# A fused hybrid block: work in front of the scan moves from GpSimd to VectorE, cross-attention queries come first, and two transposes wait longer

## The chip, the cores and the metric

The kernel runs as one launch on one core of a Trainium2 chip. The metric is the device time of that launch in microseconds. Three runs of the kernel before took 1974.82 to 1976.23 us, with a median of 1975.03 us.

## The reference, cut to what matters

One layer over 1024 tokens of width 1024, in fp32. After an RMSNorm, one large projection gives the columns of three branches and their gates.

```
h = rms_norm(x, mix_norm_w);  proj = h @ w_in
A: dn_qkv -> conv(5) -> silu -> l2-normalised q,k -> gated delta rule, both directions, chunks of 64
   (per chunk: solve a unit lower triangular system, then a scan over 16 chunks)
B: q (8 heads x 64), k, v (2 heads x 64): rms_norm per head, rotary embedding, softmax attention
     out = [x1*cos - x2*sin, x2*cos + x1*sin]
C: x_q (4 heads x 128) attends to rms_norm(mem) @ w_mem_kv   (256 memory tokens)
merged = sum over branches of sigmoid(gate) * (y_branch @ w_branch)
x = x + merged @ w_out;  x = x + relu(rms_norm(x) @ w_up)**2 @ w_down;  return rms_norm(x)
```

All of it is kept; the change alters engines, order and two constant factors that cancel.

## The kernel before, in words

Every large product is made of three fp32r matmuls: operands are split into a high half (ScalarE copy, the line 139 of `split`) and a low half (a subtraction, line 140, on VectorE, or on GpSimd where the variable `wlo[0]` is set to `gp`). `wunit` (line 144) loads a block of weights and splits it; `wtok` (line 545) does so for the token-major projections, with one buffer each for the two halves `t_hi` and `t_lo`.

A planner orders the instructions of every engine by a simulated timeline and by their place in the program; each engine then runs its own queue in order. All loads and stores named here go through the one queue of SyncE (`ld`).

Up to the scan these stages follow each other in the program, and overlap:

1. Normalise x and transpose it (lines 267 to 276). The first two weight blocks (lines 260 and 263) have their low halves on GpSimd.
2. Twelve convolution tiles (`conv_tile`, line 394), and `prep` (line 467) for eight chunk pairs, which builds the triangular matrices, multiplies them by `nbeta` on GpSimd (line 497) and stores them to `xs_d`. The gates z (`gate_z`, line 505) have low halves on GpSimd.
3. The triangular inverse: `X` is loaded (line 532), and 62 pairs of VectorE instructions (lines 726 and 727: a product into `tm`, an addition into `X`) run one after another, each on what the last one wrote. Line 729 scales the result, line 730 stores it to `ts_d`. The two instructions of step j work on (63-j)*j elements per partition, at most 992.
4. Beside it, `keys()` and `queries()` (lines 622 and 642): 24 steps. Each step projects 128 tokens into a PSUM bank `ps_dn` (four banks), and calls `rope_norm` (line 596): ScalarE copies PSUM to `x0`, GpSimd makes the products `t1` and `t2` with the cosine and sine tables (lines 604 and 605), ScalarE squares and sums each head, GpSimd raises to the power -1/2 (`rsq`, lines 135 and 136), VectorE combines (612, 613), ScalarE scales and rounds, VectorE takes the low half (618 or 620). Then TensorE transposes the result (`khl`, `qhl`; two buffers) after one more step of the other generator, ScalarE copies it out and SyncE stores it.
5. The other generator `other` (line 693): `mem_norm` (2 steps: transposes of the normalised memory `mt`, whose factor is line 572), `memory` (8 steps: keys and values of the memory), `queries_x` (8 steps: the queries of the cross-attention).
6. `gates()` (line 703) gives matmuls of the gate projections as a filler: 7 x 24 are asked for beside the scan (line 1013), 3 x 24 after it. They need nothing but weights.
7. The scan (line 760 on): `scan_pre` reads the inverse from `ts_d` into `tf` and `Tr`. Its buffers take the place of those of stage 4, so its loads start after the last of stage 4.

After the scan come softmax attention with the other gates as filler, the branch projections, the output projection and the MLP. They are not touched, but for one constant in `dn_out`.

Of the kernel before, what the change touches and what calls it, by code (L numbers as in the profile page):

```python
# [9 lines left out]
F32 = mybir.dt.float32  # L10
F32R = mybir.dt.float32r
# [8 lines left out]
P = 128  # L20
# [66 lines left out]
def hybrid_block(tc, x, mem, mix_norm_w, w_in, dn_conv_w, dn_a_log, dn_dt_bias, dn_norm_w, q_norm_w, k_norm_w,  # L87
# [168 lines left out]
        pe.matmul(ps, lhsT=one1, rhs=wrow[:, c:c + 512], start=True, stop=True)  # L256
        act.copy(out=wbc[:, c:c + 512], in_=ps)
    act.copy(out=identr, in_=ident)
    wlo[0] = gp
    first[4] = wunit(w_in[:, 4 * P:5 * P], 8, P)  # L260
    for i in range(4, 6):
        ld_rows(xts[i], x, i)
    first[0] = wunit(w_in[:, 0:P], 8, P)
    for i in range(6, 8):
        ld_rows(xts[i], x, i)
    wlo[0] = None
    for m in range(8):
        xt = xts[m]
        rs = norm_rs(xt, f"x{m}", p0)
# [9 lines left out]
    bhl = gpl.tile([P, 8, 128], F32R, name="b_hl", bufs=1)  # L279
    ld(out=braw, in_=w_in[:, C_BA:C_BA + 64].rearrange("(k p) c -> p k c", p=P))  # L280
    split(bhl[:, :, 0:64], bhl[:, :, 64:128], braw)
    ld(out=wdn, in_=dn_norm_w.rearrange("o d -> d o"))

    def proj_tok(ps, wh, wl, m):
        f, t = m // 4, slice((m % 4) * P, (m % 4 + 1) * P)
# [153 lines left out]
    for h in range(4):  # L439
        k2 = conv_tile(4 + h)  # L440
        early[0] = True
        kt = to_token(k2)
        jk = cv.tile([P, S], F32, name="c_jk", tag="c_th", bufs=1)
        ss = sml.tile([P, 8], F32, name="k_ss", tag="k_ss")
        rk = sml.tile([P, 8], F32, name="k_rk", tag="k_rk")
        act.activation(out=jk, in_=kt, func=AF.Square)
        dve.tensor_reduce(out=ss, in_=tiles(jk), axis=AX.X, op=ALU.add)
        rsq(rk, ss, 1.0, 4 * EPS)
        dve.tensor_tensor(out=tiles(kt), in0=tiles(kt), in1=bc(rk, 2, P), op=ALU.mult)
        ld(out=dram_tiles(kn_d, h), in_=tiles(kt))  # L450
        kk = to_token(kt)
        ld(out=dram_tiles(kT_d, h), in_=tiles(kk))
        q2 = conv_tile(h)
        if h == 0:
            decay()
        ld(out=dram_tiles(qT_d, h), in_=tiles(q2))
        sq = cv.tile([P, S], F32, name="c_sq", tag="c_th", bufs=1)
        act.activation(out=sq, in_=q2, func=AF.Square)
        psq = ps_dn()
        for m in range(8):  # L460
            for f in range(2):
                pe.matmul(psq[f * 64:(f + 1) * 64, 2 * m:2 * m + 2], lhsT=sq[:, m * P + (1 - f) * 64:m * P + (2 - f) * 64],
                          rhs=ones, start=True, stop=True)
        dve.tensor_scalar(out=epsq[:, :, h], in0=psq[:, 0:16].rearrange("p (m o) -> p m o", o=2)[:, :, 0],
                          scalar1=4 * EPS, scalar2=EPS * 4 * 128, op0=ALU.add, op1=ALU.mult)

    def prep(m):
        kq = pr.tile([P, 2, 4, P], F32, name="kq", tag="kq")
        ld(out=kq[:, 0], in_=kT_d[m])
        ld(out=kq[:, 1], in_=qT_d[m])  # L470
        ps = ps_dn()
        for h in range(4):
            for s in range(2):
                for f in range(2):
                    r = slice(f * 64, (f + 1) * 64)
                    pe.matmul(ps[r, s * 256 + h * 64:s * 256 + (h + 1) * 64], lhsT=kq[:, 0, h, r], rhs=kq[:, s, h, r],
                              start=True, stop=True)
        psb = ps_dn()
        for j, part in enumerate((gch, gcl)):
            rb = pr.tile([P, 2, 4, 64], F32R, name="rb", tag=f"rb{j}", bufs=1)  # L480
            gp.tensor_tensor(out=rb, in0=bc(bc(id64, 1, 4), 1, 2), in1=bc(part[:, :, m].bitcast(F32), 3, 64), op=ALU.mult)
            pe.matmul(psb, lhsT=onb, rhs=rb.rearrange("p y h c -> p (y h c)"), start=j == 0, stop=j == 1)
        df = pr.tile([P, 2, 4, 64], F32, name="df", tag="df")
        dd = pr.tile([P, 2, 2, 4, 64], F32, name="dd", tag="dd")
        dve.tensor_tensor(out=df, in0=psb.rearrange("p (y h c) -> p y h c", y=2, h=4), in1=bc(gc[:, :, m], 3, 64),
                          op=ALU.subtract)
        dve.tensor_tensor(out=dd[:, 0], in0=df, in1=bc(maskA, 2, 4), op=ALU.min)
        for y in range(2):
            dve.scalar_tensor_tensor(out=dd[:, 1, y], in0=df[:, y], scalar=ca[:, CA_SG + y:CA_SG + y + 1],
                                     in1=bc(maskX, 1, 4), op0=ALU.mult, op1=ALU.min)  # L490
        act.activation(out=dd, in_=dd, func=AF.Exp)
        qk = ps[:, 256:512].rearrange("p (h c) -> p h c", h=4)
        kk = ps[:, 0:256].rearrange("p (h c) -> p h c", h=4)
        dve.tensor_tensor(out=dd[:, 0], in0=bc(qk, 1, 2), in1=dd[:, 0], op=ALU.mult)
        ld(out=at_d[m].rearrange("p (y h) c -> p y h c", y=2), in_=dd[:, 0])
        dve.tensor_tensor(out=dd[:, 1], in0=bc(kk, 1, 2), in1=dd[:, 1], op=ALU.mult)
        gp.tensor_tensor(out=dd[:, 1], in0=dd[:, 1], in1=bc(nbeta[:, :, m], 3, 64), op=ALU.mult)
        for f in range(2):
            r = slice(f * 64, (f + 1) * 64)
            ld(out=xs_d[m, f].rearrange("a r c -> r a c"), in_=dd[r, 1].rearrange("p y h c -> p (y h) c"))  # L500
# [22 lines left out]
    for h in range(4):  # L523
# [1 line left out]
        prep(2 * h + 1)  # L525
        vt = to_token(conv_tile(8 + h))
        ld(out=dram_tiles(vn_d, h), in_=tiles(vt))
        wlo[0] = gp
        next(zs)
        wlo[0] = None  # L530
    dve.tensor_scalar(out=wdn, in0=wdn, scalar1=0.5, scalar2=None, op0=ALU.mult)
    ld(out=X, in_=xs_d.rearrange("m f a r c -> (m f a) r c"))
    for m in range(8):
        for f in range(2):
            ld(out=bcol[m * 16 + f * 8:m * 16 + f * 8 + 8], in_=bt_d[:, m, :, f])
    wlo[0] = gp
    for _ in zs:
        pass
    cst.close()
# [11 lines left out]
            split(hi[:, k:k + 4], lo[:, k:k + 4], raw, wlo[0])  # L551
        return hi, lo

    wlo[0] = gp

    mst = ExitStack()
    xp = pool(mst, "mp")
# [38 lines left out]
    def rope_norm(hi, lo, src, nh, tab, m, sc, bi):  # L596
# [3 lines left out]
        ss = sml.tile([P, 4], F32, name="r_ss", tag="r_ss")  # L600
        rs = sml.tile([P, 4], F32, name="r_rs", tag="r_rs")
        x0, t1, t2, ss, rs = x0[:, :nh], t1[:, :nh], t2[:, :nh], ss[:, :nh], rs[:, :nh]
        act.copy(out=x0, in_=src)
        gp.tensor_tensor(out=t1, in0=x0, in1=bc(tab[:, 0, m], 1, nh), op=ALU.mult)
        gp.tensor_tensor(out=t2, in0=x0, in1=bc(tab[:, 1, m], 1, nh), op=ALU.mult)
        for h in range(nh):
            act.activation(out=x0[:, h], in_=x0[:, h], func=AF.Square, accum_out=ss[:, h:h + 1])
        rsq(rs, ss, sc, bi, gp)

        def v(a, s):  # L610
# [8 lines left out]
        else:  # L619
            dve.tensor_tensor(out=lo, in0=bc(x0, 2, 2), in1=bc(hi.bitcast(F32), 2, 2), op=ALU.subtract)  # L620

    def keys():
        wh, wl = wtok(C_AKV)
        for m in range(8):
# [2 lines left out]
            vt = tkp.tile([P, 2, 64], F32, name="vt", tag="vt")  # L627
            act.copy(out=vt, in_=ps[:, 128:256].rearrange("p (g d) -> p g d", g=2))
            ld(out=vz_d[:, m], in_=vt)
            khl = tkp.tile([P, 512], F32R, name="khl", tag="qhl")[:, :384].rearrange("p (g a d) -> p g a d", g=2, a=3)  # L630
            rope_norm(khl[:, :, 1], khl[:, :, 0::2], ps[:, 0:128].rearrange("p (g d) -> p g d", g=2), 2, rope, m, 1.0 / 64, EPS)
            yield
            pst = ps_t(F32R)
            for g in range(2):
                pe.transpose(pst[:, (2 * g) * P:(2 * g + 1) * P], khl[:, g, 0:2].rearrange("p a d -> p (a d)"), identr)
                pe.transpose(pst[:, (2 * g + 1) * P:(2 * g + 2) * P], khl[:, g, 1:3].rearrange("p a d -> p (a d)"), identr)
            kab = tkp.tile([P, 512], F32R, name="kab", tag="qst").rearrange("p (g s t) -> p g s t", g=2, s=2)
            act.copy(out=kab, in_=pst.bitcast(F32).rearrange("p (g s t) -> p g s t", g=2, s=2))
            ld(out=ka_d[:, :, m * P:(m + 1) * P], in_=kab[:, :, 0])
            ld(out=kb_d[:, :, m * P:(m + 1) * P], in_=kab[:, :, 1])  # L640

    def queries():
        for g in range(2):
            wh, wl = wtok(C_AQ + g * 256)
            for m in range(8):
                ps = ps_dn()[:, :256]
                proj_tok(ps, wh, wl, m)
                qhl = tkp.tile([P, 512], F32R, name="qhl", tag="qhl").rearrange("p (h a d) -> p h a d", h=4, a=2)
                rope_norm(qhl[:, :, 0], qhl[:, :, 1], ps.rearrange("p (h d) -> p h d", h=4), 4, ropeq, m, 1.0, 64 * EPS)
                yield  # L650
                pst = ps_t(F32R)
                for h in range(4):
                    pe.transpose(pst[:, h * P:(h + 1) * P], qhl[:, h].rearrange("p a d -> p (a d)"), identr)
                qst = tkp.tile([P, 512], F32R, name="qst", tag="qst").rearrange("p (h t) -> p h t", h=4)
                act.copy(out=qst, in_=pst.bitcast(F32).rearrange("p (h t) -> p h t", h=4))
                ld(out=qs_d[4 * g:4 * g + 4, :, m * P:(m + 1) * P].rearrange("h p t -> p h t"), in_=qst)


    def queries_x():
# [30 lines left out]
                ld(out=mv_d[1][:, c - 4], in_=lo.rearrange("p (k d) -> p k d", k=2))  # L690
            yield

    other = chain(mem_norm(), memory(), queries_x())
    for _ in chain(keys(), queries()):
        next(other, None)
    for _ in other:
        pass
    mst.close()
    tst.close()
    wlo[0] = None  # L700
# [136 lines left out]
    def dn_out(m):  # L837
# [3 lines left out]
        rs = sml.tile([P, 4], F32, name="o_rs", tag="o_rs")  # L841
        act.activation(out=jk, in_=o, func=AF.Square)
        dve.tensor_reduce(out=ss, in_=jk, axis=AX.X, op=ALU.add)
        dve.scalar_tensor_tensor(out=ss, in0=ss, scalar=1.0 / 128, in1=epsq[:, m], op0=ALU.mult, op1=ALU.add)
        gp.tensor_tensor(out=rs, in0=ss, in1=mhalf[:, :4], op=ALU.pow)
        dve.tensor_tensor(out=o, in0=o, in1=bc(rs, 2, P), op=ALU.mult)
        zt = dp.tile([P, 4, P], F32, name="o_z", tag="ke")
# [416 lines left out]
```

## Time and profile before

The profiled execution took 1974.38 us by its own time, of which the traced span is 1972.7 us; 1.7 us lie around the span.

| engine | busy us | share of the span |
|---|---|---|
| TensorE matmul (PE) | 1906.1 | 97% |
| TensorE weight load (PEld) | 1611.6 | 82% |
| VectorE (DVE) | 1156.4 | 59% |
| ScalarE (ACT) | 765.1 | 39% |
| GpSimd (POOL) | 411.0 | 21% |

A view by stretches gives for each engine the time in which it was busy and, in brackets, its instructions, and behind them the TensorE clock that was granted (1.00 is full). Matmuls overlap in the pipeline: one of 512 columns is shown with 0.39 us but the next starts sooner. A view by groups gives the number of instructions, their busy time and the mean of one in ns, and then the idle time of the engine before them with what ended it.

### The profile page before, as it was taken

The page shows a single profiled execution, that of the slowest core. Times are in us where ns is not written, and L with a number is a line of the kernel's source. Part 1 is how long each engine was busy: PE and PEld are TensorE (multiplying, and loading weights), DVE is VectorE, ACT ScalarE, POOL GpSimd, SP SyncE. Part 2 cuts the span into 40 slices and gives each one's busy share as a digit, 9 for nine tenths or more (in the row PEclk, how much of TensorE's full clock was granted, in tenths as well). Part 3 has the DMA queues.
Part 4 walks back from the last instruction along what each step waited for, and adds up shares of the span by engine and source line. Part 5 has one row for each costly group of instructions (what it writes and reads, how often), then busy time and mean ns, then how long its engine had stood idle before and what let it go on. Part 6 is the DMA issues. An engine that isn't in the chain of part 4 may idle for free.

```text
span 1972.7 us, 26333 instructions
## 1 busy us (share of the span) xinstructions
PE 1906.1 (97%) x10233; PEld 1611.6 (82%) x10233; DVE 1156.4 (59%) x1665; ACT 765.1 (39%) x1547; POOL 411.0 (21%) x310
## 2 busy tenths in 40 slices
PE   6999988989999999999999999999999999999997
PEld 5887777778998888888888878888888888888886
DVE  5767899981576666666635463444443444454445
ACT  4453334445555666666642131321121212112124
POOL 2114468763251000000000520100010101001013
PEclk8999989999999999999999999999999999999999
DMA  6236644356654222222145455231111112121113
GB/s 147 76 100 184 193 146 139 113 165 188 193 164 134 86 93 76 86 75 86 59 150 200 158 179 162 76 118 42 54 54 33 53 33 64 43 65 43 43 43 86
DMA packets 232751, 207.29 MB, mean 105 GB/s; under 512 B 44785, under 2 KB 196529, under 8 KB 232114
## 3 DMA queue, kind: packets, MB, share of 16 engines
q1 hardware_dynamic: 232306, 205.08, 34.4%
q8 instruction: 81, 1.33, 0.3%
q10 hardware_dynamic: 320, 0.52, 0.1%
q14 instruction: 44, 0.36, 0.1%
HBM read 148.39 MB, written 57.18 MB: 104 GB/s over the span
## 4 chain that ended last, share of the span: by engine, by line
PE 61%; issue 12%; DVE 8%; POOL 4%; DMA 3%; ACT 2%; POOLq 0%; SPq 0%; DVEq 0%; ACTq 0%
PE ps L81 26%; PE ps_mm L81 19%; PE ps_t L84 3%; PE ps_sm L81 3%; PE ps_t L81 3%; PE ps_s L81 3%; DVE X L727 2%; PE ps_sp L81 2%; DVE tm L726 2%; POOL wdl L140 1%; PE ps_dn L81 1%; DMA w_raw<-in_w_down_dram 1%; DMA w_raw<-in_w_up_dram 1%; DMA w_raw<-in_w_out_dram 1%; POOL w_lo L140 1%
## 5 line engine op out<-in xcount | busy, mean ns | idle before, releaser
L81 PE MATMUL ps_mm<-hTh,w_hi 128*128 128x512 f32 x704 | 286.2, 407 | 6.3 <-DVE xl L140 3.2
L81 PE MATMUL ps_mm<-hTl,w_hi 128*128 128x512 f32 x704 | 284.1, 404 | 0.0
L81 PE MATMUL ps_mm<-hTh,w_lo 128*128 128x512 f32 x704 | 278.3, 395 | 0.5 <-POOL w_lo L140 0.5
L1161 DVE TENSOR_TENSOR o<-o,ps 128x512 f32<-128x512 f32 (+1 forms) x257 | 170.8, 682 | 94.7 <-PE ps L81 93.1
L140 POOL TENSOR_TENSOR wdl<-w_raw,wdh 128x1024 fp32r<-128x1024 f32 x32 | 76.4, 2397 | 602.0 <-ACT wdh L139 602.0
L81 PE MATMUL ps<-hfh,w_hi 128*128 128x512 f32 x512 | 199.4, 391 | 0.0
L81 PE MATMUL ps<-wdl,ah 128*128 128x512 f32 (+1 forms) x514 | 199.4, 388 | 0.0
L81 PE MATMUL ps<-wdh,al 128*128 128x512 f32 (+1 forms) x514 | 199.4, 388 | 0.0
L81 PE MATMUL ps<-hfl,w_hi 128*128 128x512 f32 x512 | 199.3, 389 | 0.0
L81 PE MATMUL ps<-hfh,w_lo 128*128 128x512 f32 x512 | 199.3, 389 | 0.0
L81 PE MATMUL ps<-wdh,ah 128*128 128x512 f32 (+1 forms) x514 | 188.8, 389 | 0.3 <-DVE o L1161 0.3
L1153 ACT ACTIVATE f_r<-ps 128x512 f32<-128x512 f32 x64 | 38.1, 595 | 360.9 <-PE ps L81 360.9
L140 DVE TENSOR_TENSOR w_lo<-w_raw,w_hi 128x1024 fp32r<-128x1024 f32 x78 | 100.0, 1282 | 125.9 <-ACT w_hi L139 125.2
L139 ACT CAST w_hi<-w_raw 128x1024 fp32r<-128x1024 f32 x96 | 100.9, 1051 | 174.1 <-PE ps_mm L81 92.7
L1154 DVE TENSOR_TENSOR f_r<-f_r 128x512 f32<-128x512 f32 x64 | 55.3, 864 | 183.4 <-ACT f_r L1153 183.4
L81 PEld LDWEIGHTS ps_mm<-hTh,w_hi 128*128 128x128 f32 x704 | 133.7, 190 | 31.2 <-DVE xl L140 3.4
L81 PEld LDWEIGHTS ps_mm<-hTh,w_lo 128*128 128x128 f32 x704 | 133.5, 190 | 26.1 <-POOL w_lo L140 0.7
L81 PEld LDWEIGHTS ps_mm<-hTl,w_hi 128*128 128x128 f32 x704 | 133.9, 190 | 20.7
L1093 POOL TENSOR_TENSOR g_acc<-g_acc,g_l 128x512 f32<-128x512 f32 x28 | 41.4, 1481 | 509.8 <-ACT g_yh L139 475.8
L140 DVE TENSOR_TENSOR ptl<-ps_t,pth 128x512 fp32r<-128x512 f32 x128 | 86.5, 686 | 59.9 <-ACT pth L139 59.6
L81 PEld LDWEIGHTS ps<-wdh,ah 128*128 128x128 f32 x514 | 96.4, 188 | 21.1 <-DVE o L1161 1.1
L81 PEld LDWEIGHTS ps<-wdh,al 128*128 128x128 f32 x514 | 96.5, 188 | 19.9
(292 smaller groups left out, 4081.5 us busy)
## 6 DMA issues: line engine op xcount, KB each, us to landing
w_raw<-in_w_in_dram SPq DMA_DIRECT2D x50, 512.0 KB
w_raw<-in_w_up_dram SPq DMA_DIRECT2D x32, 512.0 KB
w_raw<-in_w_down_dram SPq DMA_DIRECT2D x32, 512.0 KB
g_d<-gt SPq DMA_DIRECT2D x48, 256.0 KB
g_l<-g_d SPq DMA_DIRECT2D x24, 512.0 KB
w_raw<-in_w_branch_dram SPq DMA_DIRECT2D x12, 512.0 KB
y_raw<-y_d SPq DMA_DIRECT2D x12, 512.0 KB
xt<-in_x_dram SPq DMA_DIRECT2D x16, 256.0 KB
```

What stands on the lines that cost most here:

```text
L81: return self._put(self.tc.nc.tensor.matmul(*a, **k))
L84: return self._put(self.tc.nc.tensor.transpose(*a, **k))
L139: act.copy(out=hi, in_=src)
L140: (eng or dve).tensor_tensor(out=lo, in0=src, in1=hi.bitcast(F32), op=ALU.subtract)
L726: dve.tensor_tensor(out=t, in0=bc(X[:, j + 1:, j], 2, j), in1=bc(X[:, j, 0:j], 1, n), op=ALU.mult)
L727: dve.tensor_tensor(out=X[:, j + 1:, 0:j], in0=X[:, j + 1:, 0:j], in1=t, op=ALU.add)
L1093: (dve if bi == 2 and mt > 5 else gp).tensor_tensor(out=acc[mt][:, c], in0=acc[mt][:, c], in1=t, op=ALU.add)
L1153: act.activation(out=r, in_=ps, func=AF.Relu)
L1154: dve.tensor_tensor(out=r, in0=r, in1=r, op=ALU.mult)
L1161: dve.tensor_tensor(out=o[m][:, c], in0=o[m][:, c], in1=ps, op=ALU.add)
```

## The change

The diff, cut to its core:

```diff
@@ the first two weight blocks: low halves on VectorE @@
-    wlo[0] = gp
     first[4] = wunit(w_in[:, 4 * P:5 * P], 8, P)
...
-    wlo[0] = None
-    ld(out=wdn, in_=dn_norm_w.rearrange("o d -> d o"))
@@ prep @@
-        gp.tensor_tensor(out=dd[:, 1], in0=dd[:, 1], in1=bc(nbeta[:, :, m], 3, 64), op=ALU.mult)
+        dve.tensor_tensor(out=dd[:, 1], in0=dd[:, 1], in1=bc(nbeta[:, :, m], 3, 64), op=ALU.mult)
@@ conv, z and everything up to the scan: wlo[0] stays None @@
-        wlo[0] = gp
         next(zs)
-        wlo[0] = None
-    dve.tensor_scalar(out=wdn, in0=wdn, scalar1=0.5, scalar2=None, op0=ALU.mult)
+    ld(out=wdn, in_=dn_norm_w.rearrange("o d -> d o"))
...
-    wlo[0] = gp
@@ rope_norm @@
-        act.copy(out=x0, in_=src)
-        gp.tensor_tensor(out=t1, in0=x0, in1=bc(tab[:, 0, m], 1, nh), op=ALU.mult)
-        gp.tensor_tensor(out=t2, in0=x0, in1=bc(tab[:, 1, m], 1, nh), op=ALU.mult)
         for h in range(nh):
-            act.activation(out=x0[:, h], in_=x0[:, h], func=AF.Square, accum_out=ss[:, h:h + 1])
+            jk = tkp.tile([P, 64], F32, name="r_jk", tag="r_jk")
+            act.activation(out=jk, in_=src[:, h], func=AF.Square, accum_out=ss[:, h:h + 1])
+        dve.tensor_tensor(out=t1, in0=src, in1=bc(tab[:, 0, m], 1, nh), op=ALU.mult)
+        dve.tensor_tensor(out=t2, in0=src, in1=bc(tab[:, 1, m], 1, nh), op=ALU.mult)
@@ keys and queries: transposes are put off @@
+    turns = []
+
+    def turn(hl, nh, put):
+        def go():
+            pst = ps_t(F32R)
+            for i, part in enumerate(nh(hl)):
+                pe.transpose(pst[:, i * P:(i + 1) * P], part.rearrange("p a d -> p (a d)"), identr)
+            st = xp.tile([P, 512], F32R, name="qst", tag="qst", bufs=3)
+            act.copy(out=st, in_=pst.bitcast(F32))
+            put(st)
+        turns.append(go)
...
-                qhl = tkp.tile([P, 512], F32R, name="qhl", tag="qhl").rearrange("p (h a d) -> p h a d", h=4, a=2)
+                qhl = xp.tile([P, 512], F32R, name="qhl", tag="qhl", bufs=4).rearrange("p (h a d) -> p h a d", h=4, a=2)
...
+                turn(qhl, lambda hl: [hl[:, h] for h in range(4)], put)
                 yield
-                pst = ps_t(F32R)
...
@@ the order of the other generator, and the loop @@
-    other = chain(mem_norm(), memory(), queries_x())
-    for _ in chain(keys(), queries()):
+    other = chain(queries_x(), mem_norm(), memory())
+    for i, _ in enumerate(chain(keys(), queries())):
         next(other, None)
+        if i > 1:
+            turns.pop(0)()
     for _ in other:
         pass
+    for go in turns:
+        go()
```

The factor 0.5 on `wdn` is gone; a factor 4 in `epsq` (line 465) and in `dn_out` (line 844) stands for it.

## Rows read from the trace of the kernel before

**Rows 1.** Busy time by stretch: window, PE, PEld, DVE, ACT, POOL, clock, DMA.

```profile
236.00:436.00 200.00, 172.09 (x1067) 154.37 (x1066) 192.00 (x211) 87.72 (x290) 139.10 (x102) 0.92 0.47 142
436.00:475.00 39.00, 39.00 (x226) 33.95 (x226) 9.32 (x22) 23.00 (x95) 19.43 (x28) 1.00 0.63 196
```

**Rows 2.** What PE waited for, 170 to 480 us: total us, times, longest.

```profile
PE ps_dn L84 <- DVE mt L572: 8.4, 2, 5.6
PE ps_t L84 <- DVE khl L620: 6.3, 4, 2.2
PE ps_t L84 <- DVE qhl L618: 4.9, 6, 2.5
PE ps_mm L81 <- DVE xl L140: 3.2, 1, 3.2
```

**Rows 3.** Busy time, sum over the six stretches at half clock, 195 to 421 us.

```profile
sum 34.00, PE 28.94 PEld 26.44 DVE 33.79 ACT 10.24 POOL 23.68; mean PE 4.82 PEld 4.41 DVE 5.63 ACT 1.71 POOL 3.95
```

**Rows 4.** VectorE and GpSimd in order of time, around 250 us.

```profile
249.85 0.62 DVE L726 TENSOR_TENSOR tm<-X 128x440 f32<-128x440 f32 x1
250.51 2.70 DVE L727 TENSOR_TENSOR X<-X,tm 128x440 f32<-128x440 f32 x1
...
250.25 5.21 POOL L140 TENSOR_TENSOR t_lo<-w_raw,t_hi 128x1024 fp32r<-128x1024 f32 x2 [12.79 <-ACT t_hi L139]
```

**Rows 5.** VectorE groups by line, 170 to 436 us: count, busy us, mean ns, idle.

```profile
L727 DVE TENSOR_TENSOR X<-X,tm 128x62 f32<-128x62 f32 (+30 forms) x62 | 69.5, 1122 | 1.1
L726 DVE TENSOR_TENSOR tm<-X 128x62 f32<-128x62 f32 (+30 forms) x62 | 69.1, 1114 | 1.3
...
L613 DVE TENSOR_TENSOR r_x<-r_t,r_t 128x128 f32<-128x128 f32 (+1 forms) x18 | 11.1, 618 | 0.0
...
L620 DVE TENSOR_TENSOR khl<-r_x,khl 128x256 fp32r<-128x256 f32 x8 | 7.9, 988 | 1.2 <-ACT khl L616 1.2
L612 DVE TENSOR_TENSOR r_x<-r_t,r_t 128x128 f32<-128x128 f32 (+1 forms) x18 | 7.2, 398 | 1.8 <-ACT r_x L607 1.8
...
L140 DVE TENSOR_TENSOR mlo<-ps_mm,mhi 128x256 fp32r<-128x256 f32 x4 | 1.7, 416 | 0.0
```

**Rows 6.** VectorE in order of time, a long step with GpSimd idle.

```profile
345.08 1.19 DVE L726 TENSOR_TENSOR tm<-X 128x992 f32<-128x992 f32 x1
```

**Rows 7.** VectorE groups by line and shape, 0 to 170 us.

```profile
L140 DVE TENSOR_TENSOR w_lo<-w_raw,w_hi 128x1024 fp32r<-128x1024 f32 x8 | 9.8, 1222 | 18.7 <-ACT w_hi L139 18.4 <-PE ps_mm L81 0.3
```

**Rows 8.** GpSimd groups by line and shape, 170 to 436 us.

```profile
L140 POOL TENSOR_TENSOR w_lo<-w_raw,w_hi 128x1024 fp32r<-128x1024 f32 x15 | 40.0, 2667 | 9.6 <-ACT w_hi L139 9.6
...
L140 POOL TENSOR_TENSOR t_lo<-w_raw,t_hi 128x1024 fp32r<-128x1024 f32 x6 | 16.9, 2832 | 12.8 <-ACT t_hi L139 12.8
```

**Rows 9.** VectorE groups by line, 436 to 475 us.

```profile
L618 DVE TENSOR_TENSOR qhl<-r_x,qhl 128x256 fp32r<-128x256 f32 x6 | 2.5, 423 | 9.9 <-ACT qhl L616 9.8
...
L613 DVE TENSOR_TENSOR r_x<-r_t,r_t 128x128 f32<-128x128 f32 x6 | 1.7, 279 | 0.0
```

**Rows 10.** SyncE issues and PE in order of time, 435 to 476 us.

```profile
435.09 0.32 SPq L97 DMA_DIRECT2D ts_d<-X  x1
...
467.84 0.65 SPq L97 DMA_DIRECT2D tf<-ts_d  x1
...
475.40 0.67 PE L81 MATMUL ps_sp<-ca,tf 64*64 64x64 f32 x8
```

**Rows 11.** DMA throughput in 40 equal slices, 434 to 452 us.

```profile
GB/s 36 0 0 0 583 583 218 364 583 328 255 583 510 73 473 109 13 269 303 312 366 415 373 387 380 385 282 11 0 0 42 345 196 0 0 0 101 348 170 0
```

**Rows 12.** PE in order of time, then one group, 475 to 500 us.

```profile
470.10 0.39 PE L81 MATMUL ps_mm<-hTh,w_lo 128*128 128x512 f32 x1
470.33 0.39 PE L81 MATMUL ps_mm<-hTh,w_hi 128*128 128x512 f32 x1
...
L81 PE MATMUL ps_mm<-hTl,w_hi 128*128 128x512 f32 x18 | 7.2, 402 | 0.0
```

**Rows 13.** The gate tiles `gt`, 230 to 600 us.

```profile
L712 ACT ACTIVATE gt<-ps_mm x7: 576/591/604, 454.7 to 498.4; 128x512 f32<-128x512 f32 x7
```

More of the change, by code (lines that the diff above doesn't have):

```diff
@@ L464, in hybrid_block @@
         dve.tensor_scalar(out=epsq[:, :, h], in0=psq[:, 0:16].rearrange("p (m o) -> p m o", o=2)[:, :, 0],
-                          scalar1=4 * EPS, scalar2=EPS * 4 * 128, op0=ALU.add, op1=ALU.mult)
+                          scalar1=4 * EPS, scalar2=EPS * 16 * 128, op0=ALU.add, op1=ALU.mult)
     def prep(m):
@@ L552, in wtok @@
         return hi, lo
-    wlo[0] = gp
     mst = ExitStack()
@@ L629, in keys, with put @@
             ld(out=vz_d[:, m], in_=vt)
-            khl = tkp.tile([P, 512], F32R, name="khl", tag="qhl")[:, :384].rearrange("p (g a d) -> p g a d", g=2, a=3)
+            khl = xp.tile([P, 512], F32R, name="khl", tag="qhl", bufs=4)[:, :384].rearrange("p (g a d) -> p g a d", g=2, a=3)
             rope_norm(khl[:, :, 1], khl[:, :, 0::2], ps[:, 0:128].rearrange("p (g d) -> p g d", g=2), 2, rope, m, 1.0 / 64, EPS)
-            yield
-            pst = ps_t(F32R)
[L634 to L640, printed above, removed]
+            def put(st, m=m):
+                st = st.rearrange("p (g s t) -> p g s t", g=2, s=2)
+                ld(out=ka_d[:, :, m * P:(m + 1) * P], in_=st[:, :, 0])
+                ld(out=kb_d[:, :, m * P:(m + 1) * P], in_=st[:, :, 1])
+            turn(khl, lambda hl: [hl[:, g, s:s + 2] for g in range(2) for s in range(2)], put)
+            yield
     def queries():
@@ L647, in queries, with put @@
                 proj_tok(ps, wh, wl, m)
-                qhl = tkp.tile([P, 512], F32R, name="qhl", tag="qhl").rearrange("p (h a d) -> p h a d", h=4, a=2)
+                qhl = xp.tile([P, 512], F32R, name="qhl", tag="qhl", bufs=4).rearrange("p (h a d) -> p h a d", h=4, a=2)
                 rope_norm(qhl[:, :, 0], qhl[:, :, 1], ps.rearrange("p (h d) -> p h d", h=4), 4, ropeq, m, 1.0, 64 * EPS)
+                def put(st, g=g, m=m):
+                    ld(out=qs_d[4 * g:4 * g + 4, :, m * P:(m + 1) * P].rearrange("h p t -> p h t"),
+                       in_=st.rearrange("p (h t) -> p h t", h=4))
+                turn(qhl, lambda hl: [hl[:, h] for h in range(4)], put)
                 yield
[L651 to L656, printed above, removed]
     def queries_x():
@@ L843, in dn_out @@
         dve.tensor_reduce(out=ss, in_=jk, axis=AX.X, op=ALU.add)
-        dve.scalar_tensor_tensor(out=ss, in0=ss, scalar=1.0 / 128, in1=epsq[:, m], op0=ALU.mult, op1=ALU.add)
+        dve.scalar_tensor_tensor(out=ss, in0=ss, scalar=4.0 / 128, in1=epsq[:, m], op0=ALU.mult, op1=ALU.add)
         gp.tensor_tensor(out=rs, in0=ss, in1=mhalf[:, :4], op=ALU.pow)
```

## Prediction

> **What bounds the kernel now.** I read the shares of the engines first: TensorE is busy for 97% of the span, so a change elsewhere can only give back what TensorE loses. Next, the view by stretches, to see where it loses it. From 236 to 436 us, beside the triangular inverse, TensorE is busy for 172.1 of 200 us and VectorE for 192.0 of 200; from 436 to 475 us TensorE is busy throughout, and VectorE for 9.3 us of 39 [rows 1]. So one stretch matters, and in it two engines are close to being the limit together. The reader is to see that VectorE's 192 us are no measure of its work, since some of them are waiting (below).
>
> Third, the view of waits: TensorE stands for the normalised memory 8.4 us, for the low halves of keys 6.3 and of queries 4.9, and for the low half of a cross-attention query 3.2 [rows 2]. Fourth, the granted clock. Six stretches of 34 us together are at half of full speed, 1.2 instead of 2.4 GHz, and TensorE was busy for 28.94 us in them [rows 3]; at full clock that work takes half, so 14.5 us are lost there. Most of these stretches follow one of the waits.
>
> What does TensorE do once it is through? X is stored from 435.09, but the scan reads its inverse from 467.84 and its first matmul is at 475.40 [rows 10]: the scan waited for TensorE's queries, not for X. X has 33 us to spare. That slack is the second limit.
>
> **The change part by part, for TensorE.** *Cross-attention queries before memory:* the transposes of the memory come eight steps later, when line 572 is long done. The 8.4 us go. What comes in their place needs only weights and the projection's input. *Transposes two steps behind:* the waits for khl and qhl, 6.3 + 4.9 = 11.2 us, go, since a step's low half has another step to arrive in. Four buffers and three for the copies hold what is in flight; stores to qs_d, ka_d and kb_d are issued a step or more later on SyncE, and their readers come in the attention or in the middle of the scan. *Clock:* I take 11 of the 14.5 us as given back, since the last half-clock stretch follows the wait for xl, which nothing removes. Together 8.4 + 11.2 + 11 = 31 us for TensorE (estimate).
>
> **For VectorE, what leaves.** A long VectorE instruction with two operands in SBUF stands still while GpSimd works: the step of 440 elements took 0.62 us alone and 2.70 us beside a low half on GpSimd [rows 4]. How much of this is there? The loop's clean price: 440 elements in 0.62 us and 992 in 1.19 [rows 4, 6] give 1.03 ns per element and 0.166 us fixed. Its 62 steps have sum of (63-j)*j = 41,664 elements, so a line of the loop costs 62 x 0.166 + 41,664 x 0.00103 = 53.2 us, both lines 106.4; the groups show 69.5 + 69.1 = 138.6 [rows 5]: 32.2 us of standing still. Lines 612 and 613 at 0.28 clean [rows 9] would take 2 x 18 x 0.28 = 10.1 and show 18.3: 8.2. Line 620 at 0.423, the clean price of line 618 with as many elements [rows 9], would take 3.4 and shows 7.9: 4.5. The sum is 45 us. All of it goes if the moved operations cause it; none goes if the GpSimd operations that stay (the powers) do. Rows 4 show a moved one at work; the 21 low halves alone are 56.9 us of GpSimd [rows 8]. I take the 45, and keep zero as the other end.
>
> **For VectorE, what comes.** 15 low halves w_lo and 6 t_lo were on GpSimd between 170 and 436 us [rows 8]; some three of the 15 lie ahead of 236 in the order of the weights (estimate). 18 x 1.222 us, the price of the same subtraction on VectorE [rows 7], is 22.0. The products t1 and t2: no row has this operation, but line 140 on mlo reads one operand of 256 elements from PSUM and one from SBUF and writes as many, in a stretch in which GpSimd is busy for 139 of 200 us, at 0.416 us [rows 1, 5]. Upper bound 2.70 us as in rows 4, lower 0.28; I take the nearest, 0.416, for keys too (half as many elements, so less): 24 tiles x 2 x 0.416 = 20.0. Line 497 comes ahead of the loop, eight small products that VectorE's idle time there takes in. Nothing here is free: VectorE is the full engine. The wdn load and its halving, and the constants, are one small instruction and one small load on SyncE: nothing.
>
> [...] For 256 elements with one operand in PSUM the row shows 0.416 us, with all in SBUF 0.423 [rows 5, 9]: no difference. [...]
>
> **The two sums.** VectorE up to the end of X now: 192.0 us of 200. TensorE will be through its queries sooner, so the tail that stands behind X today goes ahead of it: six tiles, 2.5 + 2 x 1.7 = 5.9 us [rows 9]. 192.0 + 5.9 - 45 + 22.0 + 20.0 = 194.9, and 8 us of idle time as now: X ends at 236 + 203 = 439, four us later than today. From its end to the scan: the store keeps the DMA engines full until about slice 26 of 40, 434 + 26 x 0.45 = 446 us, 11 us after its issue [rows 11]; then 475.40 - 467.84 = 7.6 us from reading tf to the first matmul [rows 10]. So the scan can begin at 439 + 18.6 = 457.6 instead of 475.4: 18 us sooner. TensorE would be ready 31 us sooner. Between the two it has the seven gate tiles, which today run from about 449 to 498 (the first is evicted at 454.7, 24 matmuls of 0.23 us after its start) [rows 12, 13]: 7 x 24 x 0.23 = 39 us. Of these, 18 + 18 + 17 = 53 matmuls lie behind 475 us today [rows 12], 12 us that now come ahead of the scan and leave it. The scan's first steps use some of that as filler for their own waits, so I count half, 6 us (bounds 0 and 12). Sum: 18 + 6 = 24; with keys cheaper than 0.416 and independent instructions overlapping a little, I forecast 26 us (estimate). The profiled execution has 1974.4 us by its own time, 1.7 around its span; 1974.4 - 26 = 1948.4. It lies 0.65 us under the median of the runs, so **1949 us**.
>
> **Waits that are added.** t1 and t2 wait in VectorE's queue for the projection, and behind them stand X's next steps; as X is in the end the limit, each such wait counts. Today's idle time of 8 us contains the same kind of waits (for ScalarE), hence I keep the 8. The banks ps_dn come free after t2 rather than after one copy; four banks cover it. t_lo and w_lo come behind an X step of at most 1.2 us: TensorE may wait for weights, but it has slack of 31 against 24. ScalarE loses 24 copies. SyncE's queue is passed by weight loads in another order, of equal size. The first two blocks' low halves come between normalisations at 15 to 25 us; 2 x 1.2 us against what their presence on GpSimd costs there: zero, bounds -3 and +3.
>
> **The rivals.**
> A: *TensorE decides.* The standing still is larger than my three lines, the loop begins earlier, X is ready in time. For it: line 412 and others stand still too, uncounted. Against: VectorE is at 192 of 200. TensorE's own sum with all the clock, 8.4 + 11.2 + 14.5 + 3.2 for xl, is 37 us: 1938. [...]
> B: *A third of the standing still remains*, 15 us, from the powers on GpSimd, two instructions a tile. X ends at 454, the scan begins 3 us sooner, with the 6 of the gates 9 us: 1966.
> C: *Slower: VectorE becomes the bound.* If none of the 45 us goes, X ends at 439 + 45 = 484 and the scan begins at 502.6, 27 us late; less the 12 us of gates, 15 us slower: 1990. The point from which it decides is X ending later than about 463. For it: 42 us of new work on the fullest engine. Against: rows 4.
> D: *The change gains for TensorE nothing*, since low halves of weights now stand behind X where the transposes stood: 1975.
>
> **How the numbers follow.** Forecast 0.59, own range 1940 to 1957; A 0.16, B 0.11, C 0.08, D 0.06. What a measurement of this kernel can tell from no change is about 0.2%, 4 us. Faster: forecast, A and B, 0.86; same: D, 0.06; slower: C, 0.08. The range takes in A with 4 us and B with 2 us: 1934 to 1968; C, D and the far ends, some 0.19, are left out.
>
> **What would show it.** In the changed profile: steps of X at clean prices, both lines near 107 us; the waits for mt, khl and qhl gone; the half-clock stretches before 430 us fewer; X's end near 439 and the first ps_sp matmul near 457; no gate tile behind it. The forecast is wrong if X ends later than 463, if the loop's lines still sum to over 120 us, or if TensorE shows new waits for weights' low halves of over 10 us.

## The result, and the profile after

The changed kernel takes 1942.78 us (median of 4 runs, 1938.49 to 1945.84), the kernel before, on the same chip, 1975.63 (1974.82 to 1978.8). The ratio is 0.9829, with a 95% interval of 0.9807 to 0.9851: 1.7% faster, 33 us between the medians. The profiled execution is the slowest of the four, 1945.84 us with a span of 1944.0, and is 28.7 us shorter in its span than the one before.

In the changed file lines 732 and 733 are the loop's lines 726 and 727 of before, line 735 scales X, 599 and 600 make t1 and t2, 605 and 606 combine them. First the page's busy times (us, share of the span, instructions).

```profile
PE 1899.3 (98%) x10233; PEld 1609.5 (83%) x10233; DVE 1142.3 (59%) x1744; ACT 756.1 (39%) x1523; POOL 271.6 (14%) x230
```

The two stretches [rows 1]:

```profile
236.00:436.00 200.00, 195.59 (x1286) 178.01 (x1285) 180.59 (x296) 101.03 (x361) 51.77 (x64) 0.99 0.58 174
436.00:475.00 39.00, 34.21 (x235) 30.50 (x233) 11.78 (x21) 13.33 (x33) 5.07 (x5) 0.87 0.62 193
```

What TensorE waited for from 170 to 480 us [rows 2]:

```profile
PE ps_sp L81 <- DMA tf<-ts_d: 4.3, 1, 4.3
PE ps_mm L81 <- DVE w_lo L140: 3.0, 1, 3.0
PE ps_dn L81 <- DVE dd L493: 0.8, 1, 0.8
```

TensorE's time outside its busy time was 1972.7 - 1906.1 = 66.6 us and is 44.7: 21.9 us less. Its busy time is 6.8 us less for the same matmuls, which goes with the clock: the granted clock from 236 to 436 us is 0.99 where it was 0.92. The two make the 28.7. All rows of this view of waits together sum to 11.1 us, where they summed to 31.8. The waits for mt, khl and qhl are gone. A new one has come, for X's way through memory, and behind it 10.2 us at a granted clock of 0.50 (hence 0.87 in the second stretch).

Now VectorE's groups from 160 to 440 us [rows 5, 7, 8].

```profile
L732 DVE TENSOR_TENSOR tm<-X 128x62 f32<-128x62 f32 (+30 forms) x62 | 53.8, 868 | 5.1 <-DMA X<-xs_d 4.3
L733 DVE TENSOR_TENSOR X<-X,tm 128x62 f32<-128x62 f32 (+30 forms) x62 | 53.7, 866 | 0.8
...
L140 DVE TENSOR_TENSOR w_lo<-w_raw,w_hi 128x1024 fp32r<-128x1024 f32 x21 | 25.6, 1219 | 3.5 <-ACT w_hi L139 3.4
L140 DVE TENSOR_TENSOR t_lo<-w_raw,t_hi 128x1024 fp32r<-128x1024 f32 x6 | 7.3, 1217 | 0.0
...
L599 DVE TENSOR_TENSOR r_t<-ps_dn,ropeq 128x256 f32<-128x256 f32 x16 | 6.7, 418 | 0.0
L613 DVE TENSOR_TENSOR khl<-r_x,khl 128x256 fp32r<-128x256 f32 x8 | 3.3, 418 | 0.0
```

The handover to the scan in order of time, SyncE's issues and then TensorE [rows 10, 12]:

```profile
439.58 0.32 SPq L97 DMA_DIRECT2D ts_d<-X  x1
...
446.82 0.59 SPq L97 DMA_DIRECT2D tf<-ts_d  x1
...
445.31 0.39 PE L81 MATMUL ps_mm<-hTh,w_lo 128*128 128x512 f32 x1
449.98 1.11 PE L81 MATMUL ps_sp<-ca,tf 64*64 64x64 f32 x8 [4.28 <-DMA tf<-ts_d]
```

The loop's lines sum to 107.5 us where they were 138.6. X is stored 4.5 us later than before, yet the scan's first matmul is 25.4 us earlier, at 449.98: TensorE was through all seven gate tiles at 445.7 and then stood still until `tf` had come. Before, X lay ready and TensorE came late; now TensorE lies ready and X comes late.

### The profile page after: what moved, and what is told of

It is laid out like the page before. It is cut to its first block, busy times and chain, and to the rows that moved or that the text cites. A ratio compares the mean times of both kernels' runs of the same rounds, so it can differ in the third digit from the quotient of the medians.

```text
span 1944.0 us, 26261 instructions
## 1 busy us (share of the span) xinstructions
PE 1899.3 (98%) x10233; PEld 1609.5 (83%) x10233; DVE 1142.3 (59%) x1744; ACT 756.1 (39%) x1523; POOL 271.6 (14%) x230
## 4 chain that ended last, share of the span: by engine, by line
PE 89%; DVE 4%; DMA 3%; issue 1%; ACT 1%; SPq 0%; POOL 0%; POOLq 0%; DVEq 0%; ACTq 0%
PE ps L81 40%; PE ps_mm L81 29%; PE ps_t L84 4%; PE ps_dn L81 4%; PE ps_sm L81 3%; PE ps_t L81 3%; PE ps_s L81 3%; PE ps_sp L81 2%; DMA xt<-in_x_dram 1%; DMA xs_d<-dd 1%; DMA w_raw<-in_w_out_dram 1%; DMA X<-xs_d 1%; DVE c_acc L409 1%; DVE o L1183 0%; SPq L97 0%
## 5 line engine op out<-in xcount | busy, mean ns | idle before, releaser
L140 DVE TENSOR_TENSOR w_lo<-w_raw,w_hi 128x1024 fp32r<-128x1024 f32 x96 | 121.5, 1265 | 112.0 <-ACT w_hi L139 111.8
L81 PEld LDWEIGHTS ps_mm<-hTh,w_lo 128*128 128x128 f32 x704 | 133.6, 190 | 28.7 <-DVE w_lo L140 3.2
L81 PEld LDWEIGHTS ps<-wdl,ah 128*128 128x128 f32 x514 | 96.4, 188 | 19.8
```

Of the source, the lines that this page charges most:

```text
L81: return self._put(self.tc.nc.tensor.matmul(*a, **k))
L140: (eng or dve).tensor_tensor(out=lo, in0=src, in1=hi.bitcast(F32), op=ALU.subtract)
```

## The experiments

Two theories stood against each other. The one of the prediction: the order (cross-attention queries first, transposes two steps behind) takes TensorE's waits away, the engine moves take VectorE's standing still away, and both are needed. The rival: TensorE's waits are only VectorE's lateness, so the engine moves alone bring everything.

**The engine moves alone** (the kernel before, with the low halves, t1, t2 and line 497 on VectorE, old order and old transposes):

```
-    wlo[0] = gp            (all four places)
...
-        gp.tensor_tensor(out=t1, in0=x0, ...)
+        dve.tensor_tensor(out=t1, in0=src, ...)
```

> The engine moves alone: rotation products, nbeta product and low halves on VectorE as after the change, but the order of the other generator and the transposes as before it. My theory, two paths: X ends near 438 as after the change, both lines of its loop near 107 us, but TensorE keeps the wait for the normalised memory (8.4 us before) and part of those for khl and qhl, so its path ends later than X's: 1955 to 1962 us. Rival 1, all waits were only a result of VectorE standing still: they go by themselves and the time is that of the whole change, 1940 to 1947. Rival 2, the moves gain nothing without the order: 1970 or more.

1942.59 us, 0.9831 (0.9809 to 0.9852): the whole gain. The waits of rows 2 shrink by themselves (PE waits, 170 to 490 us):

```profile
PE ps_dn L84 <- DVE mTl L140: 3.5, 2, 2.9
PE ps_dn L84 <- DVE mt L566: 2.7, 1, 2.7
```

khl and qhl are no longer among them, although their transposes come as early as before, and all rows of the view sum to 11.5 us (31.8 before). The waits for the memory, mTl and mt, keep 6.2 us of their 8.9, but the time doesn't show it: X's way through memory decides here too (X stored at 438.0, first scan matmul at 449.3). My theory had 1955 to 1962; the rival is right. The order does bring TensorE to its gate tiles 3.7 us sooner (first eviction 411.5 in the changed kernel, 415.2 here). Those 3.7 us stand behind X; what they are worth where X no longer decides (nine gate tiles, below) was not run.

**The order alone** (the changed kernel, with the low halves, the products and line 497 back on GpSimd):

> The order alone: cross-attention queries before memory and transposes two steps behind as after the change, all engines as before it. My theory: the waits for mt, khl and qhl go (19.6 us before), the loop of X keeps its 30 us of standing still, and X, no longer behind TensorE, ends at 441 to 447 and then decides: 1953 to 1960 us. Rival 1: the order alone gives all of it, 1940 to 1947, and the engine moves are worth nothing. Rival 2: with VectorE standing still, X ends past 460 and nothing is gained: 1970 or more.

1972.73 us, 0.9978 (0.9968 to 0.9987): 0.2%, where my theory had 1953 to 1960. What TensorE waited for, 170 to 490 us:

```profile
PE ps_dn L84 <- DVE mTl L140: 6.6, 2, 6.1
PE ps_t L84 <- DVE qhl L616: 4.3, 3, 3.3
PE ps_dn L81 <- POOL t_lo L140: 3.3, 1, 3.3
PE ps_t L84 <- DVE c_x L420: 3.0, 1, 3.0
PE ps_mm L81 <- ACT w_hi L139: 2.9, 2, 2.0
...
PE ps_t L84 <- DVE khl L618: 1.6, 1, 1.6
```

VectorE's groups, the loop:

```profile
L737 DVE TENSOR_TENSOR tm<-X 128x62 f32<-128x62 f32 (+30 forms) x62 | 71.9, 1159 | 1.3
L738 DVE TENSOR_TENSOR X<-X,tm 128x62 f32<-128x62 f32 (+30 forms) x62 | 70.4, 1136 | 1.2
```

Of the gate tiles' evictions, of X's store and of the scan's first kind of matmul, shortest, median and longest in ns, first and last start:

```profile
L723 ACT ACTIVATE gt<-ps_mm x7: 589/598/604, 447.3 to 481.3; 128x512 f32<-128x512 f32 x7
...
L97 SPq DMA_DIRECT2D ts_d<-X x1: 338/338/338, 428.7 to 428.7; - x1
...
L81 PE MATMUL ps_sp<-ca,tf x128: 218/218/267, 477.0 to 584.2; 64*64 64x64 f32 x128
```

The wait for mt is gone and that for khl is down to 1.6 us, but others have grown in their place: mTl (0.5 before), t_lo (1.8), w_hi (0.3). All rows of the view sum to 29.9 us, against 31.8. What TensorE waits for is made on VectorE between the steps of its loop, and the loop is as slow as before (142.3 us, before 138.6). X is even earlier, 428.7, and the scan is not. TensorE comes to the gate tiles 7.4 us sooner than before, but still 35.8 us later than in the changed kernel, and the last of its queries are transposed and stored no sooner (468.30 against 467.39); the loads of `tf` start behind them (470.62). The order moves the places at which TensorE waits and hardly the amount.

**Which move brings it?** Low halves back on GpSimd; rotation back on GpSimd; low halves alone on the kernel before.

```
+    wlo[0] = gp            (e3: the changed kernel, at the old places)
...
-        dve.tensor_tensor(out=t1, in0=src, ...)       (e4: the changed kernel; t2, the squares likewise)
+        act.copy(out=x0, in_=src)
+        gp.tensor_tensor(out=t1, in0=x0, ...)
...
-    wlo[0] = gp            (e10: the kernel before)
```

> The changed kernel with the low halves of the weights up to the scan back on GpSimd (22 w_lo and 6 t_lo); rotation, nbeta and order as changed. My theory: VectorE loses about 26 us of work and gains some 35 us of standing still beside X, X ends at 445 to 453 against 439.5, time 1948 to 1957 us. Rival, no block between the engines: VectorE has 26 us less to do, X ends near 415 to 425 and the time is that of the whole change or 5 us less, 1935 to 1943.

> The changed kernel with the rotation products back on GpSimd behind a ScalarE copy; low halves, nbeta and order as changed. My theory: VectorE loses 18 us of work and gains 12 to 18 us of standing still; X ends within 6 us of 439.5, and the longer chain is covered by two steps: 1937 to 1948 us. Rival, the chain of a step is what counts: waits for qhl and khl come back with over 6 us, 1950 to 1960.

> The kernel before with the low halves of the weights moved to VectorE and nothing else. Theory after the first four runs, VectorE's standing still beside 2 us low halves is what TensorE waits for and the order is worth little: the loop's lines fall from 138.6 to 112 to 122 us and the time to 1945 to 1956 us. Rival, the rotation products on GpSimd hold as much, and the two only pay together: 1960 to 1970 us.

The profiled execution of e4 is the fastest of its four, 1944.73 us, 7 us under their median.

| kernel | median us | ratio to before, 95% | loop's two lines us | X stored | first scan matmul |
|---|---|---|---|---|---|
| low halves back (e3) | 1964.61 | 0.994 (0.9924 to 0.9955) | 130.3 | 441.1 | 461.2 |
| rotation back (e4) | 1952.0 | 0.9866 (0.9844 to 0.9888) | 117.4 | 434.9 | 451.1 |
| low halves alone (e10) | 1950.06 | 0.9859 (0.9843 to 0.9875) | 117.0 | 434.4 | 451.9 |

The low halves are 1.4% alone and 1.1% on top of the rest (0.994 against 0.9829); the rotation is 0.3 to 0.4% (e10 against e1, there together with line 497; e4 against the changed kernel), and there the intervals touch, so that part's size is not settled. e4 missed its 1937 to 1948 us, and not as its rival had it: the waits for khl are 1.0 us, none is for qhl.

The trace of before shows the same split step by step. Worked out from it with the prediction's clean price for each step of the loop: 21 steps that overlap a low half on GpSimd hold 22.6 us of the standing still, 30 others that overlap a rotation product 7.8, and two beside the products that make the rotation's tables 2.0. The other 71 steps, 31 of them beside the powers or another GpSimd instruction that is small or only writes, take their clean price to within 0.2 us in all.

Low halves on GpSimd cost more than was expected of e3 (1948 to 1957). Its rows tell where. The loop in VectorE's groups:

```profile
L737 DVE TENSOR_TENSOR tm<-X 128x62 f32<-128x62 f32 (+30 forms) x62 | 66.3, 1070 | 4.8 <-DMA X<-xs_d 3.8
L738 DVE TENSOR_TENSOR X<-X,tm 128x62 f32<-128x62 f32 (+30 forms) x62 | 64.0, 1032 | 0.9
```

The evictions of the gate tiles, with first and last start, here and then in the changed kernel:

```profile
L723 ACT ACTIVATE gt<-ps_mm x7: 590/597/602, 441.8 to 493.5; 128x512 f32<-128x512 f32 x7
...
L718 ACT ACTIVATE gt<-ps_mm x7: 589/597/601, 411.5 to 445.8; 128x512 f32<-128x512 f32 x7
```

The expectation went by X's end, which is only 1.5 us later than in the changed kernel. But the gate tiles begin 30 us later than there: here TensorE is the late one, waiting for operands (23.3 us in all), as in the kernel before. The profile of e4 shows the same on a smaller scale: X is stored 4.7 us sooner than in the changed kernel, and the gate tiles begin 8.8 us later, at 420.3.

**Is it the reading of SBUF by GpSimd that stops VectorE?** To the changed kernel an idle GpSimd product (a subtraction) was added that reads each new high half, 26 times from the z gates on, 16 of them within the loop's time (its result is used nowhere; views of the operands are left out here):

```
             split(hi, lo, raw, wlo[0])
+            gp.tensor_tensor(out=lockt[0], in0=hi, in1=hi, op=ALU.subtract)
```

> The changed kernel plus one idle product on GpSimd behind each weight block from the z gates to the last transposes: 1024 elements, both operands the high half in SBUF, into a tile that nobody reads. No work leaves VectorE. My theory, GpSimd reading SBUF makes a VectorE instruction with two SBUF operands stand still: both lines of X's loop grow from 107.5 to 130 to 145 us, TensorE's waits for VectorE return, time 1958 to 1975 us. Rival 1, what counted was that the low halves came late out of GpSimd, not that they held VectorE: the loop stays near 107 us and the time at 1937 to 1947 us. Rival 2, only the scan's start moves, by X ending later, and TensorE's waits stay away: 1950 to 1957 us.

1967.75 us, 0.9943 (0.9926 to 0.9959): two thirds of the gain are gone (0.57% left of 1.71), by work that nobody waits for: no row of waits names the new tile as what was waited for. The added product in GpSimd's groups from 160 us on:

```profile
L154 POOL TENSOR_TENSOR lockj<-w_hi 128x1024 f32<-128x1024 f32 x17 | 38.7, 2274 | 48.3 <-ACT w_hi L139 48.1
L553 POOL TENSOR_TENSOR lockj<-t_hi 128x1024 f32<-128x1024 f32 x6 | 14.4, 2395 | 12.9 <-ACT t_hi L139 12.6
```

One place in order of time, GpSimd and then VectorE:

```profile
299.51 2.04 POOL L154 TENSOR_TENSOR lockj<-w_hi 128x1024 f32<-128x1024 f32 x1 [4.12 <-ACT w_hi L139]
299.71 2.75 DVE L741 TENSOR_TENSOR tm<-X 128x860 f32<-128x860 f32 x1
302.49 1.05 DVE L742 TENSOR_TENSOR X<-X,tm 128x860 f32<-128x860 f32 x1
```

Two steps of 860 elements: 2.75 us beside the GpSimd product, 1.05 behind it. The loop's two lines (59.2 + 60.9) grew to 120.1 us, less than the 130 to 145 expected; VectorE's whole busy time from 170 to 446 us grew by 19.1 (246.46 to 265.55), so other instructions took the rest. X is stored 18.8 us later than in the changed kernel, and the scan begins as much later:

```profile
L97 SPq DMA_DIRECT2D ts_d<-X x1: 320/320/320, 458.4 to 458.4; - x1
...
L81 PE MATMUL ps_sp<-ca,tf x128: 218/218/367, 468.8 to 576.2; 64*64 64x64 f32 x128
```

TensorE's waits come back as well, 27.5 us against 11.1. So neither rival holds. The added load is not that of the kernel before, so the third of the gain that stays is assigned to nothing.

**Or any work of GpSimd?** The same place with two memsets, which read nothing: first into a buffer of their own, then into the weights' staging tile, so that they come when its readers are done.

```
+            gp.memset(lockt[0], 0.0)      (twice)
...
+            gp.memset(raw, 0.0)           (twice, second kernel)
```

> The changed kernel plus, at the same places, two GpSimd memsets of 1024 elements, about 2 us together, into a tile that nobody reads: GpSimd as busy as with the idle products, but it only writes. If reading is what holds VectorE: the loop's lines stay within 3 us of 107.5 and the time at 1937 to 1947 us. If any GpSimd work in SBUF holds it: as with the idle products, 130 us or more and 1955 or more.

> The changed kernel plus two GpSimd memsets of 1024 elements behind each weight block from the z gates on, now into the block's staging tile after both halves are taken, so that they run beside X's loop (the memsets of the run before had nothing to wait for and ran before 61 us). The next load into that tile waits 2 us longer. If only GpSimd's reads hold VectorE: loop lines within 3 us of 107.5, time 1938 to 1948 us. If any GpSimd work does: 115 us or more and 1955 or more.

The first (1942.13 us, 0.9825, 0.9806 to 0.9844) tells nothing of the loop: its memsets waited for nothing and ran in the first 61 us. The second took 1941.28 us, 0.982 (0.9799 to 0.9841), as the changed kernel. Its memsets in GpSimd's groups:

```profile
L153 POOL MEMSET w_raw<- 128x1024 f32 x17 | 16.2, 955 | 41.5 <-DVE w_lo L140 39.2 <-issue 2.2
```

GpSimd and VectorE in order of time around 323 us:

```profile
323.21 0.96 POOL L552 MEMSET w_raw<- 128x1024 f32 x1 [2.03 <-DVE t_lo L140]
...
323.06 1.19 DVE L742 TENSOR_TENSOR X<-X,tm 128x992 f32<-128x992 f32 x1
324.17 1.22 DVE L140 TENSOR_TENSOR t_lo<-w_raw,t_hi 128x1024 fp32r<-128x1024 f32 x1
```

1.19 us is the clean price of 992 elements [rows 6], here with a memset beside it. Worked out from the trace, 16.6 us of memsets lie beside the loop, and no step there is longer. (The loop's lines sum to 111.8 us, 4 more than in the changed kernel and 1.3 more than the 3 us that were allowed; these come in two steps beside the products for the rotation's tables, on GpSimd in both, and the kernel with split stores below has 112.1 without any memset.) So here GpSimd instructions that read large SBUF operands hold VectorE up (2.75 us against 1.05 for 128 x 860), those that only write do not (1.19 us for 128 x 992 with and without). How large an operand has to be was not tried: no step beside the small powers is longer, although they read SBUF too (128 x 4).

**What decides now?** Nine gate tiles ahead of the scan instead of seven, as cover for X's way through memory; the same with X scaled and stored in two halves; and the loop cut to 41 of 62 steps (the inverse is then incomplete), so that X comes far too early to matter.

```
-GATES = (7, 3)
+GATES = (9, 3)
...
+    for r in (slice(0, 32), slice(32, 64)):     (scaling and store of X[:, r])
...
-    for j in range(1, 63):
+    for j in range(1, 42):
```

> The changed kernel with 9 instead of 7 gate tiles asked for ahead of the scan (48 more matmuls, 11 us, which leave the end of the gates). Theory, in the changed kernel X's end decides the scan's start and TensorE stands idle for 4.3 us and then runs 10 us at half clock: both go, the first scan matmul comes within 8 us of 450 us and the time falls by 5 to 10 us, 1932 to 1939 us. Rival, those 11 us only push the scan back and the scan's own waits take nothing in: the time stays within 3 us of the changed kernel's.

> The changed kernel with 9 gate tiles ahead of the scan and X's final scaling and store in two halves of 32 rows each, so that the first store runs under the second scaling. Theory: the scan can start 3 us sooner, but TensorE has filler until about 455 us, so 0 to 3 us under the 1934.4 us of 9 gate tiles alone: 1931 to 1935 us. Rival: two stores cost more than they hide, 1935 to 1938 us.

> The changed kernel with steps 42 to 62 of the 62 of X's loop left out (the inverse is then incomplete): about 24 us less for VectorE. If X's end is what holds the scan back in the changed kernel: the first scan matmul comes 10 to 20 us sooner than 450 us, the idle time and the half clock before it go, 1930 to 1937 us. If TensorE's own work holds it: 1939 to 1945 us.

1934.42 us (0.978, 0.9766 to 0.9795), 1934.26 (0.9784, 0.9765 to 0.9803) and 1935.63 (0.9788, 0.9768 to 0.9807). With nine tiles, the stretch around the handover, and the scan's first kind of matmul:

```profile
436.00:475.00 39.00, 38.84 (x262) 33.79 (x260) 11.86 (x16) 14.21 (x33) 4.17 (x4) 1.00 0.64 202
```

```profile
L81 PE MATMUL ps_sp<-ca,tf x128: 218/218/267, 455.1 to 559.5; 64*64 64x64 f32 x128
```

TensorE is busy for 38.84 of 39 us at full clock. With the short loop, X is stored 52 us sooner:

```profile
L97 SPq DMA_DIRECT2D ts_d<-X x1: 339/339/339, 387.9 to 387.9; - x1
L81 PE MATMUL ps_sp<-ca,tf x128: 218/218/267, 427.4 to 548.5; 64*64 64x64 f32 x128
```

and the kernel gains no more than by the two tiles, although the scan begins 22.6 us sooner than in the changed kernel, more than the 10 to 20 expected: TensorE, busy for 39.00 us from 436 to 475, then has its gate tiles behind the scan's start. The 24 us taken off VectorE reach TensorE nowhere else: it is busy for 194.92 us from 236 to 436, against 195.59. So X's lateness costs the changed kernel about 8 us (1942.78 - 1934.42; 1943.76 - 1935.63 against the second run of the changed kernel, below), and nine tiles get all of it back. This version beats both kernels; its interval lies clear of the changed kernel's. The split store brings nothing beyond it, since TensorE already has work there.

**The changed kernel again**, for the spread between its runs:

> The changed kernel once more, beside the others of this call: 1939 to 1945 us. A second profile also tells whether its half-clock stretch of 10 us at the scan's start comes back.

1943.76 us (1938.82 to 1945.72 in 5 runs), 0.9827 (0.9805 to 0.9849).

## Why the prediction was right, and where it was not

- *VectorE's standing still goes, the powers on GpSimd don't keep it: right.* The loop was put at 106.4 us and took 107.5. Line by line (236 to 440 us): 31.1 from the loop, 8.9 from the 36 combining instructions (508 to 260 ns each), 4.6 from khl; 44.6 of the 45 forecast, and 2.7 more from qhl, not counted. Rival B falls: the powers (`r_rs`, 0.92 to 1.02 us each) overlap the loop for 10.5 us, worked out from the trace, and no step beside them is longer. Some standing still is left all the same: the two products for the rotation's tables stay on GpSimd (2.49 and 2.74 us, lines 586 and 587), and both instructions of line 565 beside them took 3.4 us, where the second profile has one of them at 1.28. Moving these two was not tried.
- *What comes to VectorE: right.* t1 and t2 took 0.418 us for queries (0.416 forecast) and 0.28 for keys, 17.8 us in all against 20.0; low halves in the same stretch 19.5 + 7.3, less 3.0 that were there before, 23.8 against 22.0.
- *X ends at 439: right, 439.6, but by two errors that cancel.* (The second profile of the changed kernel has X stored at 435.5, so the hit is also that of one execution.) VectorE was to be busy for 194.9 us of it and idle for 8. It was busy for 184.1 (180.59 up to 436, then 3.6) and idle for 19.4. Its groups add up to 203 us: independent instructions that start before the one ahead has ended overlap by about 18 us, worked out from the trace, 10 in the kernel before, and my sum took what came and went at full length. And it waits more, as these rows show (VectorE's waits, 236 to 440 us):

```profile
DVE tm L732 <- DMA X<-xs_d: 4.3, 1, 4.3
DVE w_lo L140 <- ACT w_hi L139: 3.4, 5, 1.3
DVE z_th L510 <- ACT z_th L509: 2.8, 1, 2.8
```

- *From X's end to the scan: the mechanism right, the size off.* I put 18.6 us there: 11 for the store, from the DMA throughput of before, and 7.6 from reading tf to the first matmul. It took 10.4: 7.2 from the store's issue to that of tf, and 3.2 to the matmul. My 11 was read from mean throughput that held other transfers too (4.23 MB in that window, of which X is 2.1), and in the 7.6 of before TensorE had gate matmuls in front. So the scan starts at 450 and not at 457.6: 25.4 us sooner instead of 18. What the profiled execution gained beside that is 3.3 us (28.7 - 25.4), where the forecast had 8.
- *The part for TensorE is the step that failed.* "The 8.4 us go" and "the waits for khl and qhl, 6.3 + 4.9 = 11.2 us, go" were credited to the order and to the transposes put off. Both went, the amount was about right (over the whole execution idle time down by 21.9, clock 6.8, together 28.7 against 31 forecast), but not for that reason: the order alone gives 0.2% and leaves 29.9 of 31.8 us of waits, the engines alone give 1.7% and leave 11.5. That the amount fits is luck: up to its last gate tile TensorE gained some 42 us (through at 445.7, against 475.4 plus the 12 us of gate matmuls that lay behind it), and the handover took part of it back, with 4.3 us idle and 10.2 us at half clock. The forecast's share for the clock was 11 of 14.5 us, on the premise that the work at half clock takes half as long at full. In the trace of before a matmul of 512 columns starts every 0.43 us at a granted clock of 0.50 (418.51 to 420.65 us) and every 0.23 at 1.00 (469.65 to 471.91), one of 256 columns every 0.21 (326.94 to 328.86) and every 0.12 (282.80 to 283.76): of the 28.94 us that saves 12.7 to 13.6 (estimate). The forecast's clocks of 1.2 and 2.4 are no reading of the profile; what it shows is that 256 more columns add 0.21 us at half clock and 0.11 at full, 1.2 and 2.4 columns per ns. Reading the row "PE ... <- DVE mt" I took the place of the wait for its cause. The cause was how late VectorE ran, and that is the 45 us.
- *Rivals.* C (VectorE the bound, 1990) asked that none of the 45 go; they went. D looked for new waits of TensorE for low halves behind X: there is one of 3.0 us for w_lo and one of 0.6 for t_lo. A was put at 1938 with TensorE deciding; the short loop shows that X still decided by 8 us, and 1934 to 1936 is what is reached when it does not. The 6 us for the gate tiles were an estimate of mine; all seven now run ahead of the scan, and what that alone gives was not measured.

The forecast, 1949, was 6 us too high. In the profiled execution (1948.4 forecast, 1945.84 measured) the scan came 7.4 us more ahead than forecast and the rest gave 4.7 less, together 2.7; the other 3 us are that this execution is the slowest of its four.

## What to carry to other kernels

When TensorE waits for results of an engine that is full, the wait's row names a place, not a cause: here moving that consumer back in the order mostly moved the wait (31.8 us of waits became 29.9), so ask first what makes the producer late. A GpSimd instruction that reads large SBUF operands beside a full VectorE can cost more than it takes off VectorE (here the low halves back on GpSimd cost 1.1%): compare its clean price there (1.22 us for a low half) with what the steps beside it lose (up to 2.1 us here) and with how much later its result comes. For the smaller rotation products the balance was not settled. After a change that frees one of two close limits, the handover to the next stage is the new place to look: here two more filler tiles were worth a quarter of the change.

## What the runs showed of the hardware that was not expected

- A memset of 128 x 1024 on GpSimd left a VectorE step with two SBUF operands at its clean time (1.19 us for 128 x 992, beside a memset of 0.96 us), while a subtraction that reads SBUF stretched one from 1.05 to 2.75 us (128 x 860). The tiny powers, which do read SBUF (128 x 4), stretched nothing that could be seen: 10.5 us of them lie beside the loop of the changed kernel.
- Two profiles of the changed kernel, with the same instructions, differ by 6.4 us in span (1944.0 and 1937.6). The longer one has a granted clock of 0.90 in its first 50 us, the shorter 1.00; the stretch at half clock at the handover is in both (0.87 from 436 to 475 us in each). Why the early stretches come in some executions was not tried, and two profiles don't settle it.
